# Feed-forward weight sums of a transformer layer: 61 of 112 made by GpSimd from blocks in SBUF, 51 by adding transfers

## The chip, the cores and the metric

One core of one Trainium2 chip runs the whole kernel. The metric is the device time of one execution in microseconds (us). TensorE multiplies; VectorE (DVE), ScalarE (ACT) and GpSimd (POOL) work element by element; SyncE (SP) issues loads. SBUF is the core's working memory of 128 partitions, PSUM holds the matmuls' sums, HBM is the memory outside the core.

## The reference

One layer of a diffusion transformer for two request groups, 128 context tokens and 512 latent tokens, 1024 features, in float32: modulation, two attention mixers, a merge, then the feed-forward part and a final norm. What the change touches is the feed-forward part:

```python
def _mlp(h, w_mlp_in, w_mlp_out):
    return jnp.square(jax.nn.relu(h @ w_mlp_in)) @ w_mlp_out
...
    h2 = _rmsnorm(x, n2) * (1 + sc2) + sh2
    return x + g2 * _mlp(h2, w1, w2)
```

`w_mlp_in` is 1024 x 4096 and `w_mlp_out` 4096 x 1024; both groups together have 640 tokens.

## The kernel before

**Layout.** Features lie on the partitions and the 640 tokens on the free axis, in two halves of 320. A weight tile is 128 output features by 1024 inputs: eight blocks of 128x128, one for each k. Each float32 operand is split into a high half (rounded for TensorE) and a low half (the rest), and a product of two operands is three matmuls for each k: high by high, high by low, low by high.

**Chunks, layers, pairs.** The 4096 hidden features are worked in four chunks c of 1024. Layer 1 makes a chunk's hidden features, layer 2 multiplies them with `w2[c]` and adds into the output tiles x. Layer 1 of chunk 0 runs in the plain way, earlier. All else, layer 1 of chunks 1 to 3 and layer 2 of chunks 0 to 3, uses a scheme of seven products instead of eight for a 2x2 by 2x2 block product. Its weights come as 28 *pairs* (l, c, n): two neighbouring weight tiles A and B, each 128x1024 (512 KB). The first four k of a tile are its first half, the last four its second. So a pair has four blocks of 128x512: A11 and A12 (the halves of tile A), A21 and A22 (the halves of tile B).

**Products and sums.** The seven products of a pair take A11, A12, A22 as they are, and four sums:

- S3 = A21 + A11 (the *first row*: A's first half is added to B's first half),
- S2 = S3 + A22 (made in place once S3 has been used),
- S4 = S2 + A12 (made in place once S2 has been used),
- S1 = A22 + A21 (made in place in B's second half once A22 has been used).

That makes 4 x 28 = 112 sums. Each is made by a transfer that adds: GpSimd issues a DMA with `accum_op=OP.add` which fetches the 256 KB of the addend from HBM again and adds it to the block in SBUF (L1401 for the first row, L1424 for the others).

**Class Operands.** `SEQ` is the list of all 196 products (l, c, n, o) in the order of TensorE. In layer 1 the products of the four n are interleaved by a list written out by hand (`FIRST1`). In layer 2 come A11 and A12 of the four n (`FIRST2`, together with the last two of layer 1), and then S3, A22, S2, S1, S4, each for n = 0 to 3.

- `feed` issues on SP the loads of the tiles in the order in which they are first needed: A tiles into `wst` (NST = 3 buffers), B tiles into `wsb` (NB = 4 buffers). After a B tile's load it issues the first row's adding transfer.
- `conv` prepares the next product's weights `wb`: ScalarE writes the high half (L1416), VectorE the low half by a subtraction (L1421); in layer 1 GpSimd does this subtraction for A12 and A22 (`BLKPOOL`, 24 products). Then it issues the adding transfer for the next sum (L1424), or frees the tile: A after A12, B after S4. For S4 in layer 2 of chunk 3 the low half is made by a transfer too (L1418, L1419).
- `ahead` lets `conv` run until six prepared weights are waiting (`W.live < 6`). The main loop takes a weight, issues its 12 matmuls (L1679 to L1681) into a PSUM bank b, calls `layer1` or `layer2` to take the result out, and calls `ahead` again.

**VectorE beside this.** It makes the low halves of the other operand (op, by `operand`, L1489 and L1486), combinations of the hidden blocks (hid, by `t_raw`, L1495 to L1501), and adds gated results to x (`gate_half`, L1532), some from a PSUM bank b, some from a temporary tp in SBUF. In chunk 3 the squares for the final norm are summed besides (acc, L1551).

Every engine works through its list in order and waits by semaphores; a scheduler sets the order of each list when the program is built.

Of the kernel before, what the change touches and what calls it, by code (L numbers as in the profile page):

```python
# [13 lines left out]
OP = mybir.AluOpType  # L14
# [60 lines left out]
def trunk_layer(ctx: ExitStack, tc: tile.TileContext, xT, small_in, wmodA, wmodB, tabs, cacheK, cacheV, bias,  # L75
                w_in, w_br, w_out, w1, w2, yT, akT, avT, bkT, bvT):
    nc = tc.nc
# [66 lines left out]
    def r32(ap):  # L144
        return ap.bitcast(F32)
# [94 lines left out]
    class Weights:  # L240
        def __init__(self):
            self.order = list(w_order())
            self.pos = {k: i for i, (k, _) in enumerate(self.order)}
            self.st, self.t = {}, {}
            self.nd = self.nc = self.live = self.busy = 0
            self.extra = self.defer = False
            self.behind = None

        def feed(self):
            while self.nd < len(self.order) and self.busy < NST:  # L250
                key, src = self.order[self.nd]
                self.st[key] = st = wp.tile([P, KT, P], F32, tag="st", bufs=NST, name="wst")
                with tc.issue_after(self.behind) if self.behind is not None and self.nd < 6 else nullcontext():
                    nc.sync.dma_start(st, src.rearrange("p (k n) -> p k n", k=KT))
                self.busy += 1
                self.nd += 1
# [902 lines left out]
    class Units:  # L1159
        n = 0  # L1160
# [209 lines left out]
    class Operands:  # L1370


        def __init__(self):
            self.st = {}
            self.loads = []
            for l, c, n, o in SEQ:
                k = (l, c, n, "A" if o in ("A11", "A12") else "B")
                if k not in self.loads:
                    self.loads.append(k)
            self.t = {}  # L1380
            self.nl = self.nc = 0
            self.busy = {"A": 0, "B": 0}

        def src(self, l, c, n, e):
            return (w1[8 * c + 2 * n + e] if l == 1 else w2[c, 2 * n + e]).rearrange("p (k n) -> p k n", k=KT)

        def feed(self):
            while self.nl < len(self.loads):
                l, c, n, x = self.loads[self.nl]
                if x == "A":  # L1390
                    if W.nd < len(W.order) or W.busy + self.busy["A"] >= NST:
                        return
                    t = wp.tile([P, KT, P], F32, tag="st", bufs=NST, name="wst")
                else:
                    if not bp or self.busy["B"] >= NB:
                        return
                    t = bp[0].tile([P, KT, P], F32, tag="sb", bufs=NB, name="wsb")
                nc.sync.dma_start(t, self.src(l, c, n, x == "B"))
                self.st[l, c, n, x] = t
                if x == "B":  # L1400
                    nc.gpsimd.dma_start(t[:, 0:4], self.src(l, c, n, 0)[:, 0:4], accum_op=OP.add)  # L1401
                self.busy[x] += 1
                self.nl += 1

        def free(self, *k):
            del self.st[k]
            self.busy[k[3]] -= 1

        def conv(self):
            self.feed()  # L1410
            l, c, n, o = SEQ[self.nc]
            k = (l, c, n, "A" if o in ("A11", "A12") else "B")
            t = self.st[k]
            t = t[:, 0:4] if o in ("A11", "S3", "S2", "S4") else t[:, 4:8]
            w = wp.tile([P, KT, P], F32R, tag="w" + "hl"[self.nc % 2], bufs=3, name="wb")
            ACT.activation(w[:, 0:4], t, AF.Copy)  # L1416
            if (l, c) == (2, 3) and (o, n) in LOTAIL:
                ACT.activation(w[:, 4:8], t, AF.Copy, scale=-1.0)  # L1418
                nc.gpsimd.dma_start(w[:, 4:8], t.bitcast(F32R), accum_op=OP.add)  # L1419
            else:  # L1420
                (nc.gpsimd if o in BLKPOOL[l - 1] else DVE).tensor_sub(w[:, 4:8], t, r32(w[:, 0:4]))  # L1421
            if o in ("S3", "S2", "A22"):
                e, half = {"S3": (1, 1), "S2": (0, 1), "A22": (1, 0)}[o]
                nc.gpsimd.dma_start(t, self.src(l, c, n, e)[:, 4 * half:4 * half + 4], accum_op=OP.add)  # L1424
            elif o in ("A12", "S4"):
                self.free(*k)
            self.t[SEQ[self.nc]] = w
            W.live += 1
            self.nc += 1
            self.feed()  # L1430
# [234 lines left out]
    for x in SEQ:  # L1665
        l, c, n, o = x
# [7 lines left out]
        whole = {"A12": "A11", "S1": "S2", "S4": "S2"}.get(o)  # L1674
# [137 lines left out]
```

## Time and profile before

| what | value |
| --- | --- |
| median of 3 runs | 916.23 us (915.66 to 916.73) |
| the profiled execution | 917.51 us |
| its span, first to last instruction | 915.7 us |
| granted TensorE clock over the span | 0.997 |
| bytes read from HBM | 137.67 MB |
| first and last matmul of the seven-product scheme | 557.5 and 905.7 us |

The page gives for each engine its busy time, its share of the span and its instruction count. A row of the windows gives for a stretch its length and then the same of PE, PEld (weight loads), DVE, ACT and POOL, the granted clock, the share of the DMA engines and GB/s. A row of the groups reads: line, engine, operation, output<-inputs, shapes, count | busy us, mean ns of one | idle time just before them and what ended it. A row of one line's records gives min/median/max in ns. A row of the timeline gives start, duration, engine, line, operation; in brackets is the idle time before it and what ended that. Matmuls overlap, so the duration of one is longer than the distance to the next.

### The profile page before, as it was taken

The numbers are of one execution on the slowest core, as the hardware profiler recorded it, in microseconds if no ns is written. First come the engines' busy times: TensorE is split into PE (matmuls) and PEld (weight loads), VectorE is DVE, ScalarE is ACT, GpSimd is POOL, SyncE is SP. The second block draws the span as 40 slices with busy tenths as digits, with TensorE's granted clock in tenths as the row PEclk, the third lists the DMA queues.
The fourth block names the chain that finished last, engine by engine and source line by source line (L and its number), as shares of the span: only waits on it lengthen the run. The fifth ranks groups of instructions, "written<-read, shape, count | busy, mean of one in ns | idle before, by whom it ended". The sixth has DMA issues, their size and how long they took to land.

```text
span 915.7 us, 16620 instructions
## 1 busy us (share of the span) xinstructions
PE 901.5 (98%) x6120; PEld 871.5 (95%) x6120; DVE 713.5 (78%) x1508; ACT 564.8 (62%) x1176; POOL 197.0 (22%) x226
## 2 busy tenths in 40 slices
PE   9999999999999999999999999999999999999996
PEld 7799989999999999999999999999999999999995
DVE  6776887757666796767789996995798769976897
ACT  4566777756667765765325667537753576357765
POOL 0020200001211011211120000354244532454140
PEclk9999999999999999999999999999999999999998
DMA  9892400126645398999743463898778876898475
GB/s 348 317 266 69 113 24 26 62 72 159 161 119 125 120 284 256 249 268 251 251 140 100 116 165 105 134 210 186 186 122 191 178 174 144 180 173 182 97 126 151
DMA packets 54465, 151.09 MB, mean 165 GB/s; under 512 B 6704, under 2 KB 10432, under 8 KB 54384
## 3 DMA queue, kind: packets, MB, share of 16 engines
q1 hardware_dynamic: 31440, 99.74, 33.1%
q0 software_dynamic: 21792, 48.98, 30.8%
q10 hardware_dynamic: 1152, 1.31, 0.4%
q8 instruction: 48, 0.79, 0.4%
q14 instruction: 33, 0.27, 0.1%
HBM read 137.67 MB, written 4.60 MB: 155 GB/s over the span
## 4 chain that ended last, share of the span: by engine, by line
PE 81%; DVE 6%; DMA 5%; ACT 4%; issue 2%; POOL 0%; SPq 0%; DVEq 0%; ACTq 0%; POOLq 0%
PE b L1680 10%; PE b L1679 10%; PE b L1681 10%; PE pg L320 7%; PE pg L321 7%; PE pg L322 7%; PE pss L322 4%; PE pss L321 4%; PE pss L320 4%; DMA wsb<-w 2%; PE pt L321 2%; PE pt L322 2%; PE pt L320 2%; DMA ms<-wmodA 2%; PE pt L710 1%
## 5 line engine op out<-in xcount | busy, mean ns | idle before, releaser
L1416 ACT ACTIVATE wb<-wsb 128x512 fp32r<-128x512 f32 x140 | 87.1, 628 | 90.6 <-PE b L1681 59.2
L1680 PE MATMUL b<-op,wb 128*128 128x320 f32 x448 | 138.6, 309 | 0.7 <-DVE op L1489 0.7
L1679 PE MATMUL b<-op,wb 128*128 128x320 f32 x448 | 138.6, 309 | 0.0
L1681 PE MATMUL b<-op,wb 128*128 128x320 f32 x448 | 138.4, 309 | 0.0
L1421 DVE TENSOR_TENSOR wb<-wsb,wb 128x512 fp32r<-128x512 f32 x124 | 92.5, 749 | 26.5 <-ACT wb L1416 26.3
L1424 POOL DMA_DIRECT2D wsb<-w x84 | 74.4, 922 | 127.8 <-DVE wb L1421 99.7
L1123 DVE SCALAR_TENSOR_TENSOR mt<-wmt,cb 128x512 f32<-128x512 f32 x128 | 80.9, 686 | 6.0 <-DMA wmt<-wmodB 6.0
L1680 PEld LDWEIGHTS b<-op,wb 128*128 128x128 f32 x448 | 84.1, 188 | 1.2 <-DVE op L1489 1.2
L1679 PEld LDWEIGHTS b<-op,wb 128*128 128x128 f32 x448 | 84.1, 188 | 0.5 <-DVE x L1532 0.4
L1681 PEld LDWEIGHTS b<-op,wb 128*128 128x128 f32 x448 | 84.1, 188 | 0.0
L272 ACT ACTIVATE wh<-wst 128x512 fp32r<-128x512 f32 (+1 forms) x84 | 61.1, 739 | 32.1 <-PE pg L321 16.6
L1401 POOL DMA_DIRECT2D wsb<-w x28 | 26.0, 930 | 138.0 <-DVE xm L341 41.5
L281 DVE TENSOR_TENSOR wl<-wst,wh 128x512 fp32r<-128x512 f32 (+1 forms) x53 | 43.3, 821 | 14.9 <-ACT wh L272 12.8
L648 DVE TENSOR_TENSOR pl<-pt,ph 128x512 fp32r<-128x512 f32 (+1 forms) x72 | 44.9, 627 | 11.8 <-ACT ph L647 11.2
L647 ACT ACTIVATE ph<-pt 128x512 fp32r<-128x512 f32 (+1 forms) x72 | 39.2, 548 | 15.7 <-PE po L718 4.7
L1532 DVE SCALAR_TENSOR_TENSOR x<-b,parts,x 128x128 f32<-128x128 f32 (+1 forms) x116 | 46.3, 429 | 2.9 <-PE b L1681 2.2
L1416 ACT ACTIVATE wb<-wst 128x512 fp32r<-128x512 f32 x56 | 34.9, 626 | 17.1 <-PE b L1681 10.3
L1679 PE MATMUL b<-t,wb 128*128 128x320 f32 x144 | 44.7, 310 | 0.0
L1681 PE MATMUL b<-t,wb 128*128 128x320 f32 x144 | 44.5, 309 | 0.0
L1680 PE MATMUL b<-t,wb 128*128 128x320 f32 x144 | 44.5, 309 | 0.0
L1489 DVE TENSOR_TENSOR op<-hid,op 128x1280 fp32r<-128x1280 f32 (+2 forms) x32 | 37.0, 1155 | 7.6 <-ACT op L1488 7.4
L1532 DVE SCALAR_TENSOR_TENSOR x<-tp,parts,x 128x320 f32<-128x320 f32 (+2 forms) x60 | 38.9, 677 | 1.0 <-ACT tp L1583 1.0
(890 smaller groups left out, 3009.2 us busy)
## 6 DMA issues: line engine op xcount, KB each, us to landing
wsb<-w POOLq DMA_DIRECT2D x112, 256.0 KB, 5.1
wst<-w SPq DMA_DIRECT2D x36, 512.0 KB, 3.9
wmt<-wmodB SPq DMA_DIRECT2D x32, 512.0 KB, 5.5
wst<-w_in SPq DMA_DIRECT2D x31, 512.0 KB, 4.4
wsb<-w SPq DMA_DIRECT2D x28, 512.0 KB, 4.0
ms<-wmodA SPq DMA_DIRECT2D x16, 512.0 KB, 8.2
wl<-w_in POOLq DMA_DIRECT2D x10, 512.0 KB, 7.6
wst<-w_br SPq DMA_DIRECT2D x8, 512.0 KB, 4.2
```

The lines of the kernel that those rows point to most:

```text
L272: ACT.activation(hi[:, ks], st[:, ks], AF.Copy)
L320: PE.matmul(ps, wh[:, k], xh[:, sl], start=first, stop=False)
L321: PE.matmul(ps, wh[:, k], xl[:, sl], start=False, stop=False)
L322: PE.matmul(ps, wl[:, k], xh[:, sl], start=False, stop=last)
L1123: DVE.scalar_tensor_tensor(t, st[:, q * 512:(q + 1) * 512], 1.0, r32(cb[2 * q + i][:, :512]), op0=OP.mult, op1=OP.mult, accum_out=parts[:, ...
L1416: ACT.activation(w[:, 0:4], t, AF.Copy)
L1421: (nc.gpsimd if o in BLKPOOL[l - 1] else DVE).tensor_sub(w[:, 4:8], t, r32(w[:, 0:4]))
L1424: nc.gpsimd.dma_start(t, self.src(l, c, n, e)[:, 4 * half:4 * half + 4], accum_op=OP.add)
L1532: DVE.scalar_tensor_tensor(X1[i][:, sl], src[:, sl.start - off:sl.stop - off], g[:, j:j + 1], X1[i][:, sl], op0=OP.mult, op1=OP.add)
L1679: PE.matmul(b, w[:, k], xh, start=not whole and k == 0, stop=False, skip_group_check=True)
L1680: PE.matmul(b, w[:, k], xl, start=False, stop=False, skip_group_check=True)
L1681: PE.matmul(b, w[:, 4 + k], xh, start=False, stop=o not in ("A11", "S2", "S1") and k == 3, skip_group_check=True)
```

## The change

First rows, the sum behind S3 and the sum behind S2 are made by `tensor_add` on GpSimd where the addend stands in SBUF at that point:

- first row (24 of 28): as soon as both tiles of the pair have been issued for loading; the other four stay transfers;
- behind S3 (25 of 28): the addend A22 is B's own second half, as long as it has not been overwritten, which is where A22 is used after S3;
- behind S2 (12 of 28, layer 1): the addend A12 is A's second half. For this an A tile of layer 1 is held until the add behind S2; before, it was freed when A12 had been prepared;
- S1's 28, the 16 behind S2 in layer 2 and 3 behind S3 stay transfers.

```diff
+            self.bare, self.used = set(), set()
...
                 nc.sync.dma_start(t, self.src(l, c, n, x == "B"))
                 self.st[l, c, n, x] = t
-                if x == "B":
-                    nc.gpsimd.dma_start(t[:, 0:4], self.src(l, c, n, 0)[:, 0:4], accum_op=OP.add)
                 self.busy[x] += 1
                 self.nl += 1
+                if x == "B":
+                    self.bare.add((l, c, n))
+                if (l, c, n) in self.bare and (l, c, n, "A") in self.st:
+                    self.first_row(l, c, n)
+
+        def first_row(self, l, c, n):
+
+            t, a = self.st[l, c, n, "B"], self.st.get((l, c, n, "A"))
+            self.bare.remove((l, c, n))
+            if a is None:
+                nc.gpsimd.dma_start(t[:, 0:4], self.src(l, c, n, 0)[:, 0:4], accum_op=OP.add)
+            else:
+                nc.gpsimd.tensor_add(t[:, 0:4], t[:, 0:4], a[:, 0:4])
...
-            t = self.st[k]
+            if o == "S3" and (l, c, n) in self.bare:
+                self.first_row(l, c, n)
+            whole = t = self.st[k]
...
-            if o in ("S3", "S2", "A22"):
+            if o == "S3" and (l, c, n, "A22") not in self.used:
+                nc.gpsimd.tensor_add(t, t, whole[:, 4:8])
+            elif o == "S2" and (l, c, n, "A") in self.st:
+                nc.gpsimd.tensor_add(t, t, self.st[l, c, n, "A"][:, 4:8])
+                self.free(l, c, n, "A")
+            elif o in ("S3", "S2", "A22"):
                 e, half = {"S3": (1, 1), "S2": (0, 1), "A22": (1, 0)}[o]
                 nc.gpsimd.dma_start(t, self.src(l, c, n, e)[:, 4 * half:4 * half + 4], accum_op=OP.add)
-            elif o in ("A12", "S4"):
+            elif o == "S4" or o == "A12" and (l == 2 or (l, c, n, "S2") in self.used):
                 self.free(*k)
+            self.used.add((l, c, n, o))
```

On PE, DVE, ACT and SP the instructions stand in the same order as before. On GpSimd they change. This is its list at layer 2 of chunk 1, from the last two first rows on; wsb_8025 to wsb_8034 are the four B tiles of the chunk's `w2`, wst an A tile. Before:

```order
L1401 DMA wsb_8031<-w2 128x512
L1401 DMA wsb_8034<-w2 128x512
L1424 DMA wsb_8025<-w2 128x512
L1424 DMA wsb_8028<-w2 128x512
L1424 DMA wsb_8031<-w2 128x512
L1424 DMA wsb_8034<-w2 128x512
```

The same six places after:

```order
L1415 TENSOR_TENSOR wsb_8030<-wsb_8030,wst_7929 128x512
L1415 TENSOR_TENSOR wsb_8033<-wsb_8033,wst_8023 128x512
L1437 TENSOR_TENSOR wsb_8025<-wsb_8025 128x512
L1437 TENSOR_TENSOR wsb_8027<-wsb_8027 128x512
L1437 TENSOR_TENSOR wsb_8030<-wsb_8030 128x512
L1437 TENSOR_TENSOR wsb_8033<-wsb_8033 128x512
```

Each issue has become an add in its own place; the first two now also wait for an A tile, and the last four read both halves of one B tile.

The second place is GpSimd's list early in layer 1 of chunk 2. The B tiles of n = 0 to 3 are wsb_8463, 8487, 8508 and 8529; wb are prepared low halves (A22 or A12). Before:

```order
L1401 DMA wsb_8508<-w1 128x512
L1424 DMA wsb_8463<-w1 128x512
L1401 DMA wsb_8529<-w1 128x512
L1424 DMA wsb_8487<-w1 128x512
L1421 TENSOR_TENSOR wb_8612<-wsb_8487,wb_8612 128x512
L1424 DMA wsb_8487<-w1 128x512
L1421 TENSOR_TENSOR wb_8629<-wst_8061,wb_8629 128x512
L1424 DMA wsb_8463<-w1 128x512
L1421 TENSOR_TENSOR wb_8685<-wst_8490,wb_8685 128x512
L1424 DMA wsb_8487<-w1 128x512
```

After:

```order
L1415 TENSOR_TENSOR wsb_8508<-wsb_8508,wst_8510 128x512
L1443 DMA wsb_8463<-w1 128x512
L1437 TENSOR_TENSOR wsb_8487<-wsb_8487 128x512
L1435 TENSOR_TENSOR wb_8611<-wsb_8487,wb_8611 128x512
L1443 DMA wsb_8487<-w1 128x512
L1435 TENSOR_TENSOR wb_8628<-wst_8060,wb_8628 128x512
L1439 TENSOR_TENSOR wsb_8463<-wsb_8463,wst_8060 128x512
L1435 TENSOR_TENSOR wb_8685<-wst_8489,wb_8685 128x512
L1415 TENSOR_TENSOR wsb_8529<-wsb_8529,wst_8667 128x512
L1439 TENSOR_TENSOR wsb_8487<-wsb_8487,wst_8489 128x512
```

The sums behind S3 and S2 stand among the subtractions as adds, and the first row of the fourth tile (wsb_8529) has moved behind them: its A tile wst_8667 takes the buffer that the add on wsb_8463 frees.

## The prediction

> **What bounds the kernel now.** I read the page first, then the windows, the records of TensorE around its gaps, the groups of VectorE and GpSimd, and last the timeline of one stretch.
>
> ```profile
> PE 901.5 (98%) x6120; PEld 871.5 (95%) x6120; DVE 713.5 (78%) x1508; ACT 564.8 (62%) x1176; POOL 197.0 (22%) x226
> 557.00:906.00 349.00, 348.29 (x2363) 346.54 (x2362) 291.79 (x492) 216.11 (x395) 130.60 (x136) 1.00 0.77 159
> 753.21 0.42 PE L1680 MATMUL b<-op,wb 128*128 128x320 f32 x1 [0.43 <-DVE op L1489]
> 852.78 0.41 PE L1680 MATMUL b<-op,wb 128*128 128x320 f32 x1 [0.28 <-DVE op L1489]
> ```
>
> TensorE sets the time. The change touches only the stretch from 557 to 906 us, where 2352 matmuls of the feed-forward products run; the second row is that window (span, then busy time and count of PE, PEld, DVE, ACT and POOL, granted clock, DMA share, GB/s). An undisturbed window of 10 us touches 70 matmuls of 0.31 us (676 to 686, below), so they follow each other by (10 + 0.31) / 70 = 0.147 us and 2363 of them need 347 us: all that TensorE loses in these 349 us is about **2 us**. No change to the sums can win more here. The last two rows are two of the gaps. The first matmul comes 0.31 + 0.43 = 0.74 us after the one before instead of 0.147, a loss of 0.59; the second loses 0.31 + 0.28 - 0.15 = 0.44; the matmul behind each is late by another 0.1. Together 1.2 us.
>
> ```profile
> 743.43 5.55 DMA wsb<-w
> 749.07 0.63 ACT wb L1416
> ```
>
> These rows of the chain of waits say why: ScalarE works in order, it stood at an adding transfer of 5.55 us, and what it converts next for that TensorE operand came late. This is what the change can cure.
>
> **What the change moves.** On PE, DVE, ACT and SP the same instructions stand in the same order. Only GpSimd's list differs: 61 of its 112 DMA issues become tensor_adds (24 first rows, 25 behind S3, 12 behind S2); four first rows and 47 others stay transfers.
>
> ```profile
> L1424 POOL DMA_DIRECT2D wsb<-w x84 | 74.4, 922 | 127.8 <-DVE wb L1421 99.7 <-ACT wb L1416 8.0 <-DVE x L1532 7.7
> wsb<-w POOLq DMA_DIRECT2D x112, 256.0 KB, 5.1
> L1421 POOL TENSOR_TENSOR wb<-wsb,wb x12: 1285/1297/1635, 600.7 to 834.3; 128x512 fp32r<-128x512 f32 x12
> L1421 POOL TENSOR_TENSOR wb<-wst,wb x12: 1294/1606/1757, 611.0 to 841.0; 128x512 fp32r<-128x512 f32 x12
> ```
>
> A sum by transfer costs GpSimd 0.92 us and is there 5.1 us later. The new instruction, a 128x512 add of two SBUF operands, has its like in the 24 subtractions that GpSimd does already: 1.29 us at least, 1.3 to 1.6 at the median. GpSimd gets 61 x 1.4 - 61 x 0.92 = 29 us more work on top of 131 in 349: it has room, and each sum is ready some 4 us sooner. The 61 x 256 KB = 16 MB less traffic is priced at nothing: the gaps above end with VectorE, and the cure of every gap is within the 2 us.
>
> **What an add costs VectorE.** GpSimd's subtractions leave a mark there:
>
> ```profile
> L1421 DVE TENSOR_TENSOR wb<-wsb,wb 128x512 fp32r<-128x512 f32 x124 | 92.5, 749 | 26.5 <-ACT wb L1416 26.3
> L1532 DVE SCALAR_TENSOR_TENSOR x<-tp,parts,x 128x320 f32<-128x320 f32 x28 | 18.5, 661 | 1.0 <-ACT tp L1583 1.0
> L1532 DVE SCALAR_TENSOR_TENSOR x<-b,parts,x 128x192 f32<-128x192 f32 x40 | 16.3, 408 | 0.0
> L1532 DVE SCALAR_TENSOR_TENSOR x<-b,parts,x 128x128 f32<-128x128 f32 x40 | 13.8, 345 | 0.4 <-PE b L1681 0.3
> L1532 DVE SCALAR_TENSOR_TENSOR x<-tp,parts,x 128x192 f32<-128x192 f32 x16 | 12.0, 752 | 0.0
> L1532 DVE SCALAR_TENSOR_TENSOR x<-tp,parts,x 128x128 f32<-128x128 f32 x16 | 10.1, 628 | 0.0
> ```
>
> The same operation on the same size takes 408 and 345 ns when one operand is the PSUM bank b, and 752 and 628 when both are SBUF tiles (tp and x). Undisturbed, a 128x512 subtraction takes 0.68 and a 128x320 x<-tp 0.55 us (rows below). The excess is 124 x 0.065 + 28 x 0.11 + 16 x 0.344 + 16 x 0.283 = 8.1 + 3.1 + 5.5 + 4.5 = 21 us, for 24 GpSimd instructions: **0.89 us of VectorE for each on the mean**. So while GpSimd adds two SBUF tiles, a VectorE instruction with two SBUF operands stands still, and one that reads PSUM does not. An adding transfer leaves no such mark: the x<-b rows and most wb are at their plain time with 112 of them about.
>
> For one new add the ends are nothing (VectorE idle or reading PSUM) and 1.29 us (VectorE back to back on SBUF operands). Whether it matters hangs on how far VectorE is ahead of TensorE where the add falls.
>
> **Where it hurts.** In layer 2 the order is S3 for four tiles, then A22, S2, S1, S4. Each S3 now puts an add into GpSimd's queue.
>
> ```profile
> 676.00:686.00 10.00, 10.00 (x70) 10.00 (x69) 10.00 (x20) 5.58 (x8) 5.42 (x7) 1.00 0.86 133
> 876.00:886.00 10.00, 10.00 (x70) 10.00 (x69) 10.00 (x18) 6.09 (x8) 5.14 (x6) 1.00 0.72 115
> ```
>
> GpSimd's issues behind the four S3 of chunk 1, and VectorE beside them (start, us, line):
>
> ```profile
> 663.31 0.86 POOL L1424 DMA_DIRECT2D wsb<-w  x1 [7.83 <-DVE wb L1421]
> 664.98 0.86 POOL L1424 DMA_DIRECT2D wsb<-w  x1 [0.81 <-DVE wb L1421]
> 668.85 0.86 POOL L1424 DMA_DIRECT2D wsb<-w  x1 [3.01 <-DVE wb L1421]
> 671.32 0.86 POOL L1424 DMA_DIRECT2D wsb<-w  x1 [1.60 <-DVE x L1532]
> 663.33 0.68 DVE L1532 SCALAR_TENSOR_TENSOR x<-b,parts,x 128x128 f32<-128x128 f32 x2 [0.32 <-PE b L1681]
> 664.00 0.69 DVE L1421 TENSOR_TENSOR wb<-wsb,wb 128x512 fp32r<-128x512 f32 x1
> 664.61 1.49 DVE L1489 TENSOR_TENSOR op<-hid,op 128x1280 fp32r<-128x1280 f32 x1
> 666.01 0.55 DVE L1532 SCALAR_TENSOR_TENSOR x<-tp,parts,x 128x320 f32<-128x320 f32 x1
> ...
> 668.47 1.48 DVE L1499 TENSOR_TENSOR hid<-hid,hid 128x1280 f32<-128x1280 f32 x1
> 669.88 0.54 DVE L1532 SCALAR_TENSOR_TENSOR x<-tp,parts,x 128x320 f32<-128x320 f32 x1
> ...
> 671.30 1.49 DVE L1489 TENSOR_TENSOR op<-hid,op 128x1280 fp32r<-128x1280 f32 x1
> 672.71 0.41 DVE L1532 SCALAR_TENSOR_TENSOR x<-b,parts,x 128x192 f32<-128x192 f32 x1
> 673.04 0.68 DVE L1421 TENSOR_TENSOR wb<-wsb,wb 128x512 fp32r<-128x512 f32 x1
> ...
> 681.03 1.49 DVE L1489 TENSOR_TENSOR op<-hid,op 128x1280 fp32r<-128x1280 f32 x1
> ```
>
> Two places where TensorE reads what VectorE has just made, one in chunk 1 (with the last row above), one in chunk 3:
>
> ```profile
> 684.41 0.31 PE L1680 MATMUL b<-op,wb 128*128 128x320 f32 x1
> 877.39 0.69 DVE L1421 TENSOR_TENSOR wb<-wsb,wb 128x512 fp32r<-128x512 f32 x1
> 878.24 0.31 PE L1681 MATMUL b<-op,wb 128*128 128x320 f32 x1
> ```
>
> The windows show VectorE without any idle time there, in chunk 1 and in chunk 3, so whatever is added shifts everything behind it. The four POOL rows are chunk 1's issues behind S3; put an add of 1.29 us in each one's place, starting when VectorE's running SBUF instruction ends. The first runs 663.31 to 664.60; the x<-b pass, the wb of 664.00 waits 0.6. The second comes amid the 1.49 us of L1489 and goes next: x<-tp waits 1.29. The third, amid L1499, the same: 1.29. The fourth goes behind the L1489 of 671.30, the x<-b passes beside it, the wb of 673.04 waits 0.95. Sum **4.1 us**, against 4 x 0.89 = 3.6 by the mean and 4 x 1.29 = 5.2 at most.
>
> The cover: the low half of the operand of S2 ends at 681.03 + 1.49 = 682.52, and the first matmul that reads it starts at 684.41, so **1.9 us** are to spare. In chunk 3, where VectorE also does the final norm's sums, the low half for the second A22 ends at 877.39 + 0.69 = 878.08, read at 878.24: **0.2 us** to spare.
>
> So TensorE waits 4.1 - 1.9 = 2.2 us in chunk 1; the same is taken for chunk 2, whose block has the same order. In chunk 0, the first-row add of the last tile also falls just ahead of the block, since its A block arrives late: 0.9 (the mean) more, 3.1. Chunk 3: 4.1 - 0.2 = 3.9. Sum 3.1 + 2.2 + 2.2 + 3.9 = 11.4 us, less 1.2 for the two cured gaps: **+10.2 us**. The profiled execution has 917.51 us (span 915.7), 1.3 over the median 916.23; from the one it makes 927.7, from the median **926.4**. By 3.6 us a block it is +8.1, by 5.2 +14.5.
>
> The Trainium skill, page "SBUF — State Buffer", section "SBUF: two separate sides", says that GpSimd shares a port pair with VectorE as an exclusive lock: "whichever ... starts first gets the pair for the whole instruction". That speaks against this change. Taken strictly each add would block the full 1.29 us and the time would be 916.23 + 14.5 = 930.7. The trace agrees on the mechanism, but its mean of 0.89 shows that part of each lock falls beside PSUM work, so I keep to the replay.
>
> **The first-layer stretch.** Some eleven new adds fall into each.
>
> ```profile
> 706.00:716.00 10.00, 10.00 (x70) 10.00 (x70) 9.96 (x13) 3.71 (x7) 6.68 (x7) 1.00 0.91 170
> 716.00:726.00 10.00, 10.00 (x70) 10.00 (x69) 6.56 (x12) 7.66 (x17) 3.95 (x4) 1.00 0.87 193
> ```
>
> They cost VectorE 11 x 0.89 = 10 us per chunk. It is full for the first 10 us and then has 3.4 in 10 idle. Two things cover it: first rows that are ready 4 us sooner, and a lead that grows again in the idle time. I take nothing, between -0.8 (the rest of the 2 us) and +2 per chunk.
>
> An A block is now held until its add behind S2, so the load of the fourth tile's A starts later, and its first-row add stands in GpSimd's queue ahead of other sums. The load lands in about 4 us and that tile is used many products later: nothing, with its end in the +2.
>
> **Rivals.**
> - *Layer 1 gives way too.* There GpSimd is busy 6.68 of 10 us and VectorE 9.96, part of it standing still; with the A load above, the low halves made by GpSimd come late. At +2 in each of three chunks: 932.4. It decides once a chunk's adds cost more than its idle time. Against it: the idle time just behind.
> - *The cover holds.* If an add costs under 0.5 us in the block (GpSimd finds the gaps, or loses the turn to VectorE), 4 x 0.5 is about the 1.9 to spare, and only chunk 3 waits a little: 916 to 917. For it: the mean is 0.89 and not 1.29. Against: no idle VectorE in the block.
> - *Faster.* ScalarE's waits for adding transfers go, TensorE wins its 2 us, and VectorE's lead covers everything: 914.2. It decides from under about 0.3 us an add, since chunk 3 has 0.2 us to spare for four of them. The gaps at 753 and 853 speak for it, chunk 3 against it.
>
> **How the numbers follow.** The forecast has 0.60, layer 1 too 0.18, the held cover 0.12, faster 0.10. A measurement of this kernel can tell about 0.2% (1.8 us) from no change. The forecast's own range is 922 to 932 (3.6 to 5.2 us a block with the ends of layer 1); with half of the held cover and most of the layer 1 case 917 to 934 leaves out about 2 in 10. Slower 0.78, same 0.12, faster 0.10.
>
> **What would show it.** GpSimd's TENSOR_TENSORs on weight blocks at 85; the wb subtractions out of wsb on VectorE well above 749 ns on the mean; in the layer 2 blocks gaps of TensorE of 2 to 4 us that end with VectorE (op or wb), the largest in chunk 3; ScalarE's waits for wsb transfers nearly gone. Wrong would be: TensorE without gaps in these blocks, gaps mainly in layer 1, or VectorE's rows unchanged.

## The result, and the profile after

| | before | after |
| --- | --- | --- |
| median of 4 runs | 916.18 us (915.66 to 916.73) | 925.44 us (924.78 to 927.52) |
| ratio, 95% interval | | 1.0093 [1.0077, 1.0109] |
| the profiled execution, and its span | 917.51 us, 915.7 us | 927.52 us, 925.4 us |
| granted TensorE clock over the span | 0.997 | 0.996 |

The change makes the kernel 0.93% slower: +9.3 us by the medians, +10.0 between the two profiled executions. The forecast was 926.4. In the kernel after, the weight preparation and the matmuls stand 14 to 20 lines lower: L1430 (was L1416, high half), L1435 (L1421, low half), L1443 (L1424, adding transfers), L1509 (L1489, op), L1552 (L1532, x), L1699 to L1701 (L1679 to L1681, the matmuls). New are the adds at L1415 (first rows), L1437 (behind S3) and L1439 (behind S2).

From the page of the kernel after, its busy times and its groups:

```profile
PE 905.0 (98%) x6120; PEld 872.0 (94%) x6120; DVE 750.6 (81%) x1508; ACT 565.4 (61%) x1176; POOL 240.4 (26%) x226
L1430 ACT ACTIVATE wb<-wsb 128x512 fp32r<-128x512 f32 x140 | 86.7, 627 | 73.9 <-PE b L1701 55.4
L1435 DVE TENSOR_TENSOR wb<-wsb,wb 128x512 fp32r<-128x512 f32 x124 | 108.6, 880 | 12.4 <-ACT wb L1430 12.1
L1415 POOL TENSOR_TENSOR wsb<-wsb,wst 128x512 f32<-128x512 f32 x24 | 34.7, 1446 | 112.1 <-DMA wst<-w 78.5
L1443 POOL DMA_DIRECT2D wsb<-w x47 | 41.2, 892 | 39.8 <-DVE wb L1435 16.5
L1437 POOL TENSOR_TENSOR wsb<-wsb 128x512 f32<-128x512 f32 x25 | 40.4, 1617 | 41.4 <-DVE wb L1435 41.4
```

VectorE has as many instructions as before (1508) and 37 us more busy time: the same 124 subtractions last 880 ns on the mean instead of 749. GpSimd is 43 us busier. The waits of TensorE at the matmuls of the feed-forward products, kernel after (us in all, times, longest):

```profile
PE b L1701 <- DVE wb L1435: 3.5, 8, 0.9
PE b L1699 <- DVE x L1552: 1.4, 2, 0.9
PE b L1699 <- DVE tp L1538: 0.4, 2, 0.2
PE b L1700 <- DVE op L1509: 0.3, 1, 0.3
```

All four end with VectorE. The windows of two of the four layer-2 blocks, first from the kernel before, then from the kernel after:

```profile
660.00:700.00 40.00, 40.00 (x275) 40.00 (x274) 38.30 (x68) 21.49 (x32) 12.88 (x15) 1.00 0.76 149
860.00:905.00 45.00, 45.00 (x304) 44.35 (x303) 42.83 (x80) 34.35 (x64) 13.86 (x16) 1.00 0.59 94
```

```profile
660.00:700.00 40.00, 38.49 (x258) 37.48 (x257) 37.84 (x61) 21.66 (x34) 15.85 (x13) 1.00 0.45 89
860.00:905.00 45.00, 42.71 (x288) 41.91 (x287) 42.69 (x72) 30.71 (x54) 17.30 (x17) 1.00 0.41 72
```

In the same 40 us TensorE starts 17 matmuls fewer (17 x 0.147 = 2.5 us), in the 45 us 16 fewer. VectorE is as busy as before and gets 7 and 8 fewer instructions done: it is stretched, not idle. (The blocks start 2.7 and 6.0 us later in the kernel after, so the windows don't hold quite the same instructions.) The share of the DMA engines falls from 0.76 to 0.45, and that is worth nothing here: no_l2s3 below has 45 transfers fewer and wins nothing.

**The block of chunk 1, kernel after** (the timeline: start, duration, engine; GpSimd's adds first, then VectorE, then TensorE's gaps):

```profile
661.04 1.30 POOL L1415 TENSOR_TENSOR wsb<-wsb,wst 128x512 f32<-128x512 f32 x1 [7.45 <-DMA wst<-w]
667.23 1.31 POOL L1437 TENSOR_TENSOR wsb<-wsb 128x512 f32<-128x512 f32 x1 [4.89 <-DVE wb L1435]
669.16 2.48 POOL L1437 TENSOR_TENSOR wsb<-wsb 128x512 f32<-128x512 f32 x1 [0.63 <-DVE wb L1435]
674.07 2.48 POOL L1437 TENSOR_TENSOR wsb<-wsb 128x512 f32<-128x512 f32 x1 [2.44 <-DVE wb L1435]
677.58 1.30 POOL L1437 TENSOR_TENSOR wsb<-wsb 128x512 f32<-128x512 f32 x1 [1.03 <-DVE wb L1435]
...
661.62 1.26 DVE L1435 TENSOR_TENSOR wb<-wst,wb 128x512 fp32r<-128x512 f32 x1 [1.91 <-ACT wb L1430]
...
667.82 1.25 DVE L1435 TENSOR_TENSOR wb<-wsb,wb 128x512 fp32r<-128x512 f32 x1
669.00 1.48 DVE L1509 TENSOR_TENSOR op<-hid,op 128x1280 fp32r<-128x1280 f32 x1
670.40 1.58 DVE L1552 SCALAR_TENSOR_TENSOR x<-tp,parts,x 128x320 f32<-128x320 f32 x1
...
675.31 1.58 DVE L1552 SCALAR_TENSOR_TENSOR x<-tp,parts,x 128x320 f32<-128x320 f32 x1
...
677.68 2.55 DVE L1509 TENSOR_TENSOR op<-hid,op 128x1280 fp32r<-128x1280 f32 x1
...
681.21 0.41 PE L1701 MATMUL b<-op,wb 128*128 128x320 f32 x1 [0.52 <-DVE wb L1435]
683.80 0.41 PE L1701 MATMUL b<-op,wb 128*128 128x320 f32 x1 [0.56 <-DVE wb L1435]
686.20 0.42 PE L1701 MATMUL b<-op,wb 128*128 128x320 f32 x1 [0.38 <-DVE wb L1435]
```

This is the replay of the prediction, almost add by add. An add that begins while VectorE runs no instruction with two SBUF operands takes 1.3 us, and the subtraction that comes up beside it lasts 1.25 instead of 0.68 (the first L1437, the L1435 of 667.82). One that is issued amid the 1.48 us of L1509 takes 2.48: it waits until that ends (669.00 + 1.48 = 670.48, and 670.48 + 1.2 is its own end), and then the x<-tp behind L1509 lasts 1.58 instead of 0.55. The engines take turns, and each turn holds the other up. The four adds cost VectorE 0.6 + 1.0 + 1.0 + 1.1 = 3.7 us (4.1 predicted); the last first row, ahead of the block, another 0.6.

### The profile page after: what moved, and what is told of

Read it like the earlier page. It is cut to its first block, busy times and chain, and to the rows that moved or that the text cites. A ratio compares the mean times of both kernels' runs of the same rounds, so it can differ in the third digit from the quotient of the medians.

```text
span 925.4 us, 16516 instructions
## 1 busy us (share of the span) xinstructions
PE 905.0 (98%) x6120; PEld 872.0 (94%) x6120; DVE 750.6 (81%) x1508; ACT 565.4 (61%) x1176; POOL 240.4 (26%) x226
## 3 DMA queue, kind: packets, MB, share of 16 engines
q0 software_dynamic: 13008, 32.98, 19.4%
## 4 chain that ended last, share of the span: by engine, by line
PE 69%; DVE 17%; ACT 5%; DMA 4%; issue 3%; POOL 1%; SPq 0%; DVEq 0%; ACTq 0%; POOLq 0%
PE b L1701 7%; PE b L1699 7%; PE b L1700 7%; PE pg L320 6%; PE pg L321 6%; PE pg L322 6%; PE pss L322 4%; PE pss L321 4%; PE pss L320 4%; DVE wb L1435 3%; PE pt L321 2%; PE pt L322 2%; PE pt L320 2%; DVE op L1509 2%; DMA wst<-w 2%
## 5 line engine op out<-in xcount | busy, mean ns | idle before, releaser
L1701 PE MATMUL b<-op,wb 128*128 128x320 f32 x448 | 139.2, 311 | 3.5 <-DVE wb L1435 3.5
L1699 PE MATMUL b<-op,wb 128*128 128x320 f32 x448 | 138.7, 310 | 1.4 <-DVE x L1552 1.4
L1430 ACT ACTIVATE wb<-wsb 128x512 fp32r<-128x512 f32 x140 | 86.7, 627 | 73.9 <-PE b L1701 55.4
L1435 DVE TENSOR_TENSOR wb<-wsb,wb 128x512 fp32r<-128x512 f32 x124 | 108.6, 880 | 12.4 <-ACT wb L1430 12.1
L1701 PEld LDWEIGHTS b<-op,wb 128*128 128x128 f32 x448 | 84.1, 188 | 5.6 <-DVE wb L1435 5.6
L1699 PEld LDWEIGHTS b<-op,wb 128*128 128x128 f32 x448 | 84.1, 188 | 2.3 <-DVE x L1552 2.3
L1415 POOL TENSOR_TENSOR wsb<-wsb,wst 128x512 f32<-128x512 f32 x24 | 34.7, 1446 | 112.1 <-DMA wst<-w 78.5
L648 DVE TENSOR_TENSOR pl<-pt,ph 128x512 fp32r<-128x512 f32 (+1 forms) x72 | 44.9, 626 | 11.8 <-ACT ph L647 11.4
L1443 POOL DMA_DIRECT2D wsb<-w x47 | 41.2, 892 | 39.8 <-DVE wb L1435 16.5
L1437 POOL TENSOR_TENSOR wsb<-wsb 128x512 f32<-128x512 f32 x25 | 40.4, 1617 | 41.4 <-DVE wb L1435 41.4
L1552 DVE SCALAR_TENSOR_TENSOR x<-b,parts,x 128x128 f32<-128x128 f32 (+1 forms) x116 | 45.9, 423 | 0.3 <-PE b L1701 0.3
L1552 DVE SCALAR_TENSOR_TENSOR x<-tp,parts,x 128x320 f32<-128x320 f32 (+2 forms) x60 | 46.0, 796 | 0.0
L1435 DVE TENSOR_TENSOR wb<-wst,wb 128x512 fp32r<-128x512 f32 x44 | 39.4, 899 | 8.1 <-ACT wb L1430 8.0
L1699 PE MATMUL b<-t,wb 128*128 128x320 f32 x144 | 44.7, 310 | 0.4 <-DVE tp L1538 0.4
L1509 DVE TENSOR_TENSOR op<-hid,op 128x1280 fp32r<-128x1280 f32 (+2 forms) x32 | 41.4, 1294 | 4.1 <-ACT op L1508 4.0
L1430 ACT ACTIVATE wb<-wst 128x512 fp32r<-128x512 f32 x56 | 34.6, 625 | 16.5 <-PE b L1701 8.9
```

The lines of the kernel that those rows point to most:

```text
L1509: DVE.tensor_sub(lo, src, r32(hi))
L1552: DVE.scalar_tensor_tensor(X1[i][:, sl], src[:, sl.start - off:sl.stop - off], g[:, j:j + 1], X1[i][:, sl], op0=OP.mult, op1=OP.add)
L1699: PE.matmul(b, w[:, k], xh, start=not whole and k == 0, stop=False, skip_group_check=True)
L1701: PE.matmul(b, w[:, 4 + k], xh, start=False, stop=o not in ("A11", "S2", "S1") and k == 3, skip_group_check=True)
```

## Where TensorE loses its time

Each kernel below was timed beside the kernel before on the same chip, where that had a median of 916.2 to 918.5 us. For every run the loss of TensorE is added up from the starts of the 2352 matmuls: what the distance between two of them has above 0.147 us, where it is over 0.165. "Blocks" are the last 24 products of a chunk's layer 2 (in chunk 3 without its last five products, where every kernel loses 1.1 to 1.2 us, before too); "layer 1" is all between. "Stalls" is what VectorE's instructions last beyond the usual time of their kind (the lower quartile of line, output and shape; only over 0.1 us, and from 557 us on). The time comes from four to twelve runs of each kernel; losses and stalls come from the one trace of each.

| kernel | adds by GpSimd | time against before, 95% | blocks, us | layer 1, us | stalls, us |
| --- | --- | --- | --- | --- | --- |
| before | none | | 0.1 | 1.7 | 21.3 |
| after | 61 | 1.0093 [1.0077, 1.0109] | 8.0 | 2.5 | 61.7 |
| l2s3_only | 16 behind S3, layer 2 | 1.0138 [1.0112, 1.0163] | 6.8 | 9.1 | 34.1 |
| no_l2s3 | the other 45 | 1.0001 [0.9986, 1.0015] | 0.2 | 1.3 | 45.1 |
| idle_adds | 16 that nobody needs | 1.0152 [1.0128, 1.0175] | 7.9 | 9.0 | 34.8 |
| idle_sets | none, 48 memsets | 1.0037 [1.0026, 1.0049] | 1.0 | 3.6 | 19.6 |
| rows_only | 24 first rows | 1.0099 [1.0060, 1.0138] | 0.0 | 10.9 | 31.7 |
| rows_but_4th | 21 first rows | 0.9992 [0.9980, 1.0004] | 0.0 | 0.5 | 31.0 |
| no_rows | 37: S3 and S2 | 1.0160 [1.0145, 1.0175] | 7.6 | 8.4 | 46.1 |
| rows_l2s3 | 24 rows + the 16 | 1.0242 [1.0225, 1.0260] | 6.0 | 17.3 | 41.0 |
| rows21_l2s3 | 21 rows + the 16 | 1.0117 [1.0092, 1.0142] | 7.3 | 6.5 | 52.6 |
| s2_only | 12 behind S2 | 0.9996 [0.9986, 1.0006] | 0.0 | 0.7 | 27.3 |
| rows21_s2 | 21 rows + 12 behind S2 | 0.9999 [0.9989, 1.0009] | 0.4 | 1.3 | 40.6 |
| l2s3_dve | none, the 16 by VectorE | 1.0183 [1.0168, 1.0198] | 3.2 | 14.2 | 19.4 |

Two columns tell the story. The blocks lose 6 to 8 us in each of the six kernels with 16 adds in layer 2, and under half a microsecond in each kernel with neither those nor the memsets nor VectorE's own sums. The stalls alone decide nothing: no_l2s3 has 45 us of them, twice those of before, and loses no time that can be told.

## The experiments

Two theories stood at the start. **A**, the prediction's: a GpSimd add of SBUF tiles stops VectorE (the port), and in a layer-2 block VectorE has no time to give. **B**: what costs is GpSimd's own list, its waits for held A tiles and its longer occupation, so that transfers behind an add are issued late. In all kernels but the last (l2s3_dve), PE, DVE, ACT and SP have the same lists in the same order as before.

### The 16 sums in layer 2, alone and taken out

`l2s3_only` is the kernel before with

```diff
-            t = self.st[k]
+            whole = t = self.st[k]
...
-            if o in ("S3", "S2", "A22"):
+            if o == "S3" and l == 2:
+                nc.gpsimd.tensor_add(t, t, whole[:, 4:8])
+            elif o in ("S3", "S2", "A22"):
```

> The kernel before, with only the 16 sums behind S3 in layer 2 made by GpSimd. Theory A (an add of two SBUF tiles stops VectorE, which has no idle time in the layer 2 blocks): these 16 are the main part, about +7.5 us over before (the gaps of TensorE in the four layer 2 blocks of the changed kernel sum to 7.8), gaps of 1 to 3 us in each block, VectorE's wb<-wsb mean up. Theory B (the held A tiles and GpSimd's longer queue make weights late): 0 to +1 us, because no A tile is held and no first row is moved.

`no_l2s3` is the kernel after without them:

```diff
-            if o == "S3" and (l, c, n, "A22") not in self.used:
+            if o == "S3" and l == 1 and (l, c, n, "A22") not in self.used:
```

> The changed kernel, with those 16 sums put back to adding transfers; the other 45 adds stay on GpSimd. Theory A: the layer 2 gaps go, what is left is the 1.3 us of layer 1 and up to 1 us at the start and the end, so +1 to +2.5 us over before. Theory B: A tiles are still held and first rows still moved, so about +8 us over before.

Measured: 931.80 us beside 917.95, +13.8; and 918.16, +0.2, which rules out B's +8 and lies under A's +1 to +2.5. The 16 adds are the whole loss, and more: alone they cost more than with the other 45. A's +7.5 fits what the blocks lose (6.8 us, 8.0 in the full change) and misses the time, since layer 1 now loses 9.1 us. The chain there, from ScalarE's timeline in layer 1 of chunk 2 (the longest waits) and the waits of TensorE, kernel l2s3_only:

```profile
711.31 0.63 ACT L1416 ACTIVATE wb<-wsb 128x512 fp32r<-128x512 f32 x1 [5.80 <-DMA wsb<-w]
718.35 0.63 ACT L1416 ACTIVATE wb<-wsb 128x512 fp32r<-128x512 f32 x1 [3.02 <-DMA wsb<-w]
```

```profile
PE b L1681 <- DVE tp L1520: 4.1, 3, 2.0
```

VectorE leaves the block late, so the B tiles come free late, and the first rows of layer 1 are transferred late (counted from the first matmul of chunk 1's block, the next B tile's load is issued after 31.6 us instead of 28.3 before, and its first row after 35.5 instead of 32.4); ScalarE stands for them, VectorE stands for ScalarE, takes the results out late, and TensorE waits for a PSUM bank. That is a follow-on of A that I had left out.

### The port or GpSimd's list?

`idle_adds` keeps all 112 transfers and adds 16 sums into a tile that nobody reads:

```diff
+            if o == "S3" and l == 2:
+                zz = bp[0].tile([P, 4, 128], F32, tag="zz", bufs=1, name="zz")
+                nc.gpsimd.tensor_add(zz, r32(w[:, 4:8]), self.st[k][:, 4:8])
```

> The kernel before with all its 112 transfers, and 16 idle adds: behind each S3 in layer 2 GpSimd adds the low half of wb and the second half of the B tile into a spare tile that nobody reads. No sum is ready sooner and no tile is held longer. Theory A: the port alone does it, +6 to +9 us, with the gaps in the same four blocks. Theory B: about 0, at most +1 for the 1.3 us that GpSimd's next issue is later.

`idle_sets` has in the place of that add

```diff
+                nc.gpsimd.tensor_copy(zz[:, 0, 0:1], r32(w[:, 4, 0:1]))
+                for i in range(3):
+                    nc.gpsimd.memset(zz, 0.0)
```

> Before with all its 112 transfers, and at each of the 16 sums behind S3 in layer 2 a one-column copy out of wb and three memsets of a 128x512 tile that nobody reads, on GpSimd: it is kept busy there for about as long as by the idle adds (three times some 0.45 us), but reads next to nothing from SBUF. Port theory (VectorE stands only beside a GpSimd instruction that reads SBUF): 0 to +1 us. If the idle adds' +15 us came from GpSimd's own list being busy, so that its transfers are issued later: +10 to +16 us.

Measured: +14.9 us (932.85 beside 917.95; A's +6 to +9 fits the 7.9 us lost in the blocks, and layer 1 loses 9.0 besides, as in l2s3_only), and +3.8 (921.02 beside 917.23; by the ratio 2.4 to 4.5). GpSimd and VectorE's subtractions in the groups of idle_adds, then of idle_sets:

```profile
L1424 POOL TENSOR_TENSOR zz<-wb,wsb 128x512 f32<-128x512 f32 x16 | 27.9, 1742 | 61.1 <-DVE wb L1421 61.1
L1421 DVE TENSOR_TENSOR wb<-wsb,wb 128x512 fp32r<-128x512 f32 x124 | 96.7, 785 | 35.4 <-ACT wb L1416 35.4
```

```profile
L1426 POOL MEMSET zz<- 128x512 f32 x48 | 31.7, 661 | 1.8
L1421 DVE TENSOR_TENSOR wb<-wsb,wb 128x512 fp32r<-128x512 f32 x124 | 92.1, 746 | 32.2 <-ACT wb L1416 32.0
```

And the window of chunk 1's block, idle_adds, then idle_sets:

```profile
660.00:700.00 40.00, 38.58 (x260) 37.81 (x258) 37.40 (x63) 21.66 (x34) 17.50 (x16) 1.00 0.66 128
```

```profile
660.00:700.00 40.00, 40.00 (x275) 40.00 (x274) 37.77 (x68) 22.85 (x36) 18.92 (x29) 1.00 0.73 145
```

With memsets GpSimd is busier in the block (18.92 us against 17.50), and yet VectorE does its 68 instructions and TensorE its 275 matmuls, as before. With adds whose result nobody needs VectorE does 63 and TensorE 260. So what stops VectorE is not that GpSimd works but that it reads SBUF beside it. This is what the Trainium skill says, page "SBUF — State Buffer", section "Who interferes with whom": a VectorE instruction with two SBUF inputs is in the way of a GpSimd instruction that reads SBUF, not of one that only writes it. The trace agrees: stalls of 19.6 us with memsets, 34.8 with adds, 21.3 before. My 0 to +1 for the memsets was too low: the busy list (31.7 us of memsets and 16 copies, more than the 27.9 of the adds) goes with some 2 us more lost in layer 1 and 1 in the blocks. If that is theory B's part, it is about a quarter of the 14.9; no run shows it by itself.

### First rows alone: theory B's wait

`rows_only` is the kernel after without the sums behind S3 and S2, and without held A tiles:

```diff
-            if o == "S3" and (l, c, n, "A22") not in self.used:
-                nc.gpsimd.tensor_add(t, t, whole[:, 4:8])
-            elif o == "S2" and (l, c, n, "A") in self.st:
-                nc.gpsimd.tensor_add(t, t, self.st[l, c, n, "A"][:, 4:8])
-                self.free(l, c, n, "A")
-            elif o in ("S3", "S2", "A22"):
+            if o in ("S3", "S2", "A22"):
...
-            elif o == "S4" or o == "A12" and (l == 2 or (l, c, n, "S2") in self.used):
+            elif o in ("A12", "S4"):
```

> The kernel before with only the 24 first rows made by GpSimd (no A tile held). Theory A: they fall where VectorE has idle time or before it is behind, 0 to +2 us, some of it in chunk 0 where the last one falls ahead of the block. Theory B: first rows wait for the A tile's load and block GpSimd's queue, +2 to +5 us with waits of GpSimd for wst.

Measured: 928.70 us, +10.8, and all of it in layer 1. A misses; B's wait is there, and three of the four runs pass its +5. The four spread more than those of any other kernel here, along with the granted clock: 923.16 us at 0.997, the value of before, and 927.76, 929.65 and 930.75 at 0.993, 0.993 and 0.991. So the one run with the clock of before lost 5.2 us. The rest goes along with stretches at half clock behind TensorE's pauses; the trace, of the run of 927.76, has two (last section). GpSimd's timeline in layer 1 of chunk 2, then ScalarE's and TensorE's, kernel rows_only:

```profile
719.71 1.84 POOL L1415 TENSOR_TENSOR wsb<-wsb,wst 128x512 f32<-128x512 f32 x1 [4.21 <-DMA wst<-w]
721.50 0.87 POOL L1438 DMA_DIRECT2D wsb<-w  x1
...
725.58 1.15 ACT L1430 ACTIVATE wb<-wsb 128x512 fp32r<-128x512 f32 x2 [2.62 <-DMA wsb<-w]
...
727.78 0.42 PE L1694 MATMUL b<-t,wb 128*128 128x320 f32 x1 [1.78 <-DVE tp L1533]
```

The add for the fourth tile waits 4.21 us for its A tile, and the transfer behind it, for another tile that is needed sooner, is not issued before 721.50. A transfer for the first row needs no A tile and waits for nothing of the kind. `rows_but_4th` gives back only these three:

```diff
+                if x == "B" and l == 1 and n == 3:
+                    nc.gpsimd.dma_start(t[:, 0:4], self.src(l, c, n, 0)[:, 0:4], accum_op=OP.add)
-                if x == "B":
+                elif x == "B":
                     self.bare.add((l, c, n))
```

> The first rows alone by GpSimd (24, of which three in layer 1, those of the fourth tile n = 3, are transfers again: 21 adds). With all 24 this cost 10 us, all of it in layer 1. If the loss came from GpSimd's list standing at the fourth tile's add until its A tile had landed (4.2 us at 720 us), with the next transfers behind it: 0 to +1.5 us. If it came from VectorE's stalls by the adds: some +8 to +10, since only three adds go.

Measured: 917.47 beside 917.60, nothing. VectorE's stalls are the same (31.0 us, 31.7 in rows_only) and the 10 us are gone. So they came with these three adds and not with the stalls. A late A tile does no harm as such: in rows_but_4th other first rows still wait for theirs, eight of them 2.2 to 7.6 us, and nothing is lost. In the rows of rows_only the harm is that a sum stands behind the add that ScalarE needs sooner: it stands 2.62 us for it at 725.58.

### What keeps layer 1 whole in the full change

`no_rows` is the kernel after with all first rows as transfers:

```diff
                 if x == "B":
-                    self.bare.add((l, c, n))
-                if (l, c, n) in self.bare and (l, c, n, "A") in self.st:
-                    self.first_row(l, c, n)
+                    nc.gpsimd.dma_start(t[:, 0:4], self.src(l, c, n, 0)[:, 0:4], accum_op=OP.add)
```

> The change without its first rows: 24 first rows are transfers again, 37 adds stay (25 behind S3, 12 behind S2). With all 61 the layer-1 stretches lose little though the 16 adds of layer 2 alone make them lose some 6 us. If it is the first rows, ready sooner, that mend layer 1: about the +13.8 of the 16 adds alone. If it is the adds behind S3 and S2 of layer 1: +8 to +10, as with all 61.

`rows_l2s3` is rows_only with the two lines of l2s3_only; `rows21_l2s3` is rows_but_4th with them.

> Before with two parts: all 24 first rows and the 16 sums behind S3 in layer 2 by GpSimd; the sums behind S2, and those behind S3 in layer 1, stay transfers. First rows alone +10, the 16 alone +14. If first rows as adds mend what the late block does to layer 1, but the transfers in front of the fourth tile's add leave its queue wait: about +15 to +20 (the block's +8 and the queue's +10, a little overlapping). If nearly all is mended as in the full change: +8 to +10. If the two add up: +24.

> Before with the 16 sums behind S3 in layer 2 and 21 first rows by GpSimd; the fourth tile's first row in layer 1 is a transfer again, as are the sums behind S2 and those behind S3 in layer 1. The 16 alone cost +14, these 21 rows alone nothing, the 16 with all 24 rows +22. If first rows as adds mend what a late layer-2 block does to the layer-1 stretch behind it: +7 to +9, the full change's value. If the mending needs the adds behind S2 and S3 as well: +12 to +15.

Measured: no_rows +14.7 (932.34 beside 917.60), rows_l2s3 +23.1 (940.33 beside 917.23) and rows21_l2s3 +11.1 (929.58 beside 918.46), between its two expectations. In rows_l2s3 the block's loss and the queue's loss add up (13.8 + 10.8 = 24.6 against 23.1; by the ratios 1.38 + 0.99 = 2.37% against 2.42%). Without first rows by GpSimd the mending is gone (no_rows). With 21 of them and no other sum a part of it is there in the trace, 6.5 us lost in layer 1 instead of 9.1; the times alone don't tell the two apart, since the intervals of l2s3_only and rows21_l2s3 overlap. ScalarE's wait for wsb transfers goes the same way. The groups of l2s3_only, no_rows, rows21_l2s3 and after, each with what ended its idle time:

```profile
L1416 ACT ACTIVATE wb<-wsb 128x512 fp32r<-128x512 f32 x140 | 85.8, 626 | 95.1 <-PE b L1683 47.3 <-DMA wsb<-w 40.9 <-DVE x L1534 2.7
```

```profile
L1428 ACT ACTIVATE wb<-wsb 128x512 fp32r<-128x512 f32 x140 | 86.2, 627 | 83.4 <-PE b L1699 44.8 <-DMA wsb<-w 31.7 <-DVE x L1550 3.2
```

```profile
L1432 ACT ACTIVATE wb<-wsb 128x512 fp32r<-128x512 f32 x140 | 86.2, 627 | 81.0 <-PE b L1700 51.7 <-DMA wsb<-w 25.1 <-issue 1.6
```

```profile
L1430 ACT ACTIVATE wb<-wsb 128x512 fp32r<-128x512 f32 x140 | 86.7, 627 | 73.9 <-PE b L1701 55.4 <-DMA wsb<-w 13.6 <-DVE x L1552 3.3
```

40.9, 31.7, 25.1, 13.6 us of waiting, with 9.1, 8.4, 6.5 and 2.5 us lost in layer 1. So the change mends in layer 1 most of what it breaks there by leaving the block late: neither the first rows alone nor the sums behind S3 and S2 alone do it. Which of these two sums does more wasn't separated. Why the fourth tile's wait is harmless in the full change: in GpSimd's list (the second place shown under The change) an add behind S2 now stands ahead of it, and the wait is 1.95 us instead of 4.21:

```profile
720.88 1.30 POOL L1439 TENSOR_TENSOR wsb<-wsb,wst 128x512 f32<-128x512 f32 x1 [2.44 <-DVE wb L1435]
722.14 1.75 POOL L1435 TENSOR_TENSOR wb<-wst,wb 128x512 fp32r<-128x512 f32 x1
725.85 1.34 POOL L1415 TENSOR_TENSOR wsb<-wsb,wst 128x512 f32<-128x512 f32 x1 [1.95 <-DMA wst<-w]
727.15 1.29 POOL L1439 TENSOR_TENSOR wsb<-wsb,wst 128x512 f32<-128x512 f32 x1
```

The sum behind it at 727.15 is done 1.29 us later, where a transfer takes 5.3 us to land (the median in the kernel after); that this is what makes the 1.95 us harmless follows from these rows but wasn't tried by itself.

### The harmless parts together

`s2_only` is the kernel before with the adds behind S2 and the A tiles held for them:

```diff
-            if o in ("S3", "S2", "A22"):
+            if o == "S2" and (l, c, n, "A") in self.st:
+                nc.gpsimd.tensor_add(t, t, self.st[l, c, n, "A"][:, 4:8])
+                self.free(l, c, n, "A")
+            elif o in ("S3", "S2", "A22"):
...
-            elif o in ("A12", "S4"):
+            elif o == "S4" or o == "A12" and (l == 2 or (l, c, n, "S2") in self.used):
```

`rows21_s2` is that with the first rows of rows_but_4th.

> Before, with one part of the change alone: the 12 sums behind S2 in layer 1 made by GpSimd, with the A tiles held until then; first rows and the sums behind S3 stay transfers. Port theory: 12 adds of 0.7 to 0.9 us, four in each chunk and none in a layer-2 block, in stretches where VectorE has idle time: -1 to +1 us. Held tiles and queue waits: the A tiles are held longer, and the first rows that are transfers don't wait for A, so also about 0 to +1; only a loss of several us would speak for the held tiles.

> The parts that cost nothing alone, together: 21 first rows (not those of the fourth tile in layer 1) and the 12 sums behind S2 by GpSimd, all behind S3 as transfers. No add falls into a layer-2 block, no first row stands in the queue for a late A tile. If the gaps of TensorE at 753 and 853 us are cured as each part alone cured them: -1 to -0.5 us, near what can be told; if not, 0. More than -2 is not to be had.

Measured: 916.85 and 917.54, beside 917.60 and 917.23: no difference in either. Held A tiles cost nothing that can be told. The gaps at 753 and 853 are gone in s2_only's trace and smaller in rows21_s2's (0.2 and 0.3 us), with others in their place; the two lose 1.9 and 3.0 us in all, before 3.1. No version here beats the kernel before by more than can be told.

### The same 16 sums by VectorE

`l2s3_dve` is l2s3_only with `DVE.tensor_add(t, t, whole[:, 4:8])`. The lists of VectorE, ScalarE and TensorE change their order with it.

> Before, with the 16 sums behind S3 in layer 2 made by VectorE itself (tensor_add in its own list, 0.68 us each), so that no GpSimd add stops it. Port theory: the loss goes by how much of VectorE's time each sum takes in the block: 4 x 0.68 = 2.7 us a block instead of 4 x 0.89, less the 1.9 us of cover in chunks 0 to 2: +3 to +8 us, with what follows in layer 1, under the +13.8 of the same 16 sums by GpSimd. If the loss came from GpSimd's list or from ready times of the sums, it would be about 0.

Measured: 934.16 beside 917.60, +16.6; the expectation misses by far. The sums take 0.68 us each (16 x 0.68 = 10.9 us), and the blocks lose 3.2 us, fewer than with GpSimd's adds, as they should. But layer 1 loses 14.2. How much of that is VectorE leaving the block late and how much the other order of its list wasn't separated.

## Why the prediction was right, point by point

The forecast, +10.2, stood 0.9 us over the measured +9.3, for the reason that it gave. Its terms were less exact than its sum: that the errors of the terms nearly cancelled is luck.

- **Where it hurts.** Right, and shown: no loss without the 16 adds in the blocks, and the same block loss with adds that do nothing.
- **What an add costs VectorE.** 0.89 us was taken for each. The 16 alone: (34.1 - 21.3) / 16 = 0.80; the idle ones (34.8 - 21.3) / 16 = 0.84. Over all 61 it is (61.7 - 21.3) / 61 = 0.66, and over the 45 of no_l2s3 (45.1 - 21.3) / 45 = 0.53. These stop VectorE too, and cost no time.
- **The blocks: 11.4 predicted, 8.0 measured.** By chunk 3.1, 2.2, 2.2, 3.9 predicted; 1.1, 2.6, 1.1, 3.1 measured. Two sizes were off. VectorE's stalls in the four blocks are 3.1, 3.7, 3.4 and 3.0 us, 13.3 in all, where the replay had 16.4. And I counted the last first row ahead of the block for chunk 0 alone; it stands there in all four, 0.6 to 0.7 us each, 2.5 in all. Together 15.8, of which 15.8 - 8.0 = 7.8 was covered, not 5.9. The cover was read from one pair of rows in chunk 1 and taken over to 0 and 2. It came out at 2.7, 1.7, 2.9 and 0.5 us for chunks 0 to 3, against 1.9, 1.9, 1.9 and 0.2.
- **Which wait.** For chunks 0 to 2 I named the low half of op for S2. TensorE comes late one step earlier, at A22, and there it waits for the weights' low halves (the wb rows above; once, by 0.2 us, for op). In chunk 3 I named the weights' low half for the second A22, and that is one of its gaps (1.0 us at 887). The two others are a third thing, a PSUM bank that VectorE had not taken out yet, kernel after:

```profile
869.32 2.22 DVE L1509 TENSOR_TENSOR op<-hid,op 128x1280 fp32r<-128x1280 f32 x1
...
872.47 0.54 DVE L1552 SCALAR_TENSOR_TENSOR x<-b,parts,x 128x320 f32<-128x320 f32 x1
...
873.06 0.42 PE L1699 MATMUL b<-op,wb 128*128 128x320 f32 x1 [0.88 <-DVE x L1552]
```

  The x<-b pass is at its plain time (0.54), but it stands in VectorE's list behind an L1509 that lasted 2.22 instead of 1.49. An instruction need not be stopped itself to be late.
- **The cured gaps: -1.2 predicted.** Not had: the two gaps shrink only to 0.6 and 0.3 us (at 758 and 858), others come up, and layer 1 with all of them loses 2.48 us instead of 1.75, +0.7. ScalarE's waits for wsb transfers, which I had "nearly gone", fell from 22.7 to 13.6 us.
- **The sum in the profiled executions:** blocks +7.8, layer 1 +0.7; the first matmul 0.5 later (in the other runs it starts anywhere from 557.3 to 558.6), and 0.6 behind the last one: 9.6, which is what the two spans differ by; 0.4 of the 10.0 measured lies outside the spans. The 3.6 us too many in the blocks were balanced by the 1.9 that the gaps and layer 1 gave less, and the 1.1 ahead and behind, of which the forecast said nothing.
- **Held A tiles and the fourth first row: nothing.** True of the full change, but the reason I gave (that tile is used many products later) was wrong: what counts is not the tile that waits but the sums queued behind it, +10.8 us in rows_only.
- **The rivals.** *Layer 1 gives way too*: with parts of the change it does, by 5 to 16 us, though by late first rows and by waits in GpSimd's list rather than by late low halves. In the full change the mending holds it to 0.7. *The cover holds* and *faster* fell in the blocks; the ceiling of 2 us on any gain stood in every run.

## What to carry to other kernels

Before moving work to GpSimd because it has room, look at what VectorE does at that very place: an add of 1.3 us over SBUF tiles cost VectorE some 0.8 us where it runs back to back, and 0.5 us elsewhere, where idle time made up for it. So the same instruction was free in 45 places and cost 14 us in 16. Look then at the queue: an add that needs a second tile waits for it in order, and everything behind it on GpSimd waits too; a transfer from HBM in its place did not wait. And try the parts of a change alone and together, since here they did not always add up: 14 and 0 made 9, while 14 and 11 made 23.

## What the hardware showed unexpectedly

**Half the clock after a pause.** Some of TensorE's pauses of over 2 us were followed by a stretch at half speed: matmuls 0.267 us apart instead of 0.147. The windows around such a pause, kernel rows_l2s3:

```profile
731.00:734.00 3.00, 0.70 (x6) 0.44 (x4) 1.49 (x3) 1.27 (x3) 1.64 (x2) 1.00 0.92 178
734.00:737.00 3.00, 3.00 (x12) 3.00 (x13) 0.69 (x1) 2.02 (x5) 1.08 (x2) 0.50 1.08 254
737.00:742.00 5.00, 5.00 (x35) 5.00 (x34) 2.37 (x4) 3.57 (x7) 1.12 (x2) 0.96 0.61 132
```

The granted clock is 0.50 in the second row: 12 matmuls in 3 us instead of 20, at least 1.2 us lost again. The traces have six such stretches inside the feed-forward products, each 3.41 us long: two in rows_l2s3 (from 734.0 and 839.8), two in rows_only (728.8 and 831.2), one in l2s3_only (626.5) and one in l2s3_dve (834.9). They came after pauses (start to start) of 2.1 to 2.6 us. Others of 2.1 to 3.0 us had no such stretch behind them (2.7 in idle_adds at 831, 2.2 in no_rows at 726 and 829, 3.0 in rows_l2s3 at 623), nor had any trace without a pause over 2 us, the full change among them.

What decides is where a pause falls. The two stretches of rows_l2s3 begin 105.8 us apart and those of rows_only 102.4, which is 31 and 30 times 3.413; in all four kernels the drop of the clock at the kernel's end lies a whole number of such steps later. So in these traces the clock changes only on steps of 3.413 us. In the step just ahead of the six stretches TensorE started 6 to 9 matmuls (a full step holds 23) and was busy, by the profile, for 32 to 48% of it. Of the steps with no half clock behind them, the emptiest in the same part of all traces had 9 (one, in rows_only, 45% busy) and 10 (51%). So the bound lies near 9 starts, and is not exactly known. The Trainium skill, page "TensorE: Matmul & The Clock Gate", section "What's actually happening", has the clock halved after an idle window of about 3.4 us and whole again after a busy one of that length, with windows that run freely. The traces agree on the length and on the free-running windows; they add that such a window need not be idle throughout.

**The price of GpSimd's instructions beside VectorE.** A 128x512 add takes 1.3 us when VectorE runs no instruction with two SBUF inputs as it starts, and up to 2.49 when it is issued amid one; a memset of the same tile takes 0.53 us at the median, without a mark on VectorE (stalls of 19.6 us with 48 of them, 21.3 without).
